# A hybrid decoder layer on one core: the cross output projection by seven block products, block sums per token tile, five early gate products, and the cross query through DRAM

## The chip, the core and the metric

The kernel runs on one core of a Trainium2 chip. The core has TensorE (PE, with the load of its stationary operand counted apart as PEld), VectorE (DVE), ScalarE (ACT) and GpSimd (POOL), each with an instruction queue that is worked off in order. SyncE (SP) issues nearly all DMAs, from one more such queue: an issue waits until its source is written and its destination is free, and what stands behind it waits too. The metric is the device time of one execution in microseconds; the time of a kernel is the median of its runs.

## What is computed

One layer of a decoder trunk on 1024 tokens of width 1024, f32, with three sub-layers, each between two RMSNorms. The change begins in the second and reaches into the third:

```python
h = h + rmsnorm(mixed @ w_out, norm_mix_post)
hn = rmsnorm(h, norm_x_pre)
qx = (hn @ w_q_x).reshape(b, s, X_HEADS, X_HEAD_DIM)              # 4 heads of 256
kx, vx = jnp.split(mn @ w_kv_x, 2, axis=-1)                        # 256 memory tokens
...
px = jax.nn.softmax(sx, axis=-1)
ox = jnp.einsum("bhsm,bmhd->bshd", px, vx).astype(h.dtype).reshape(b, s, D_MODEL)
h = h + rmsnorm(ox @ w_o_x, norm_x_post)
hn = rmsnorm(h, norm_ffn_pre)
g, up = jnp.split(hn @ w_gate_up, 2, axis=-1)                      # 2 x 2816 columns
h = h + rmsnorm((jax.nn.silu(g) * up) @ w_down, norm_ffn_post)
```

## The kernel before

**Matmuls.** Every f32 product is made of three matmuls on split operands (`mm3`, L60 to L62): high times high, high times low, low times high. `split` (L66, L75) makes the two parts of an operand tile: ACT rounds the high part, DVE subtracts it from the source. So each new operand of PE costs an ACT step and a DVE step behind it. A tile that has tokens in its rows is turned by PE transposes (`turn_in`, tiles `ptr`) and split into `A_h` and `A_l`, which hold the layer's current operand for all 1024 tokens, 8 blocks of 128 columns.

**Seven products.** Where two 2x2 block matrices are multiplied, the kernel forms seven products of sums of blocks in place of eight plain ones. Before the change the gate and up products (each pair of a gate and an up column tile is one `unit`, L1247) and the down products (L1357 on) are made so; the cross output projection isn't.

**The stages around the change**, in the order of the program:

- Query products (`qx_mm`, L996): 16 tiles `pqx` of 128 columns and 512 tokens. `qx_evac` (L1024) splits each from PSUM into `qxh` and `qxl`, which stay on the chip, as do the split keys `kxh`, `kxl` and values `vxh`, `vxl`.
- Cross attention: eight pieces (4 heads by two halves of the tokens) go through `x_scores` (`psx`, L1048), `x_soft`, `x_turn` and `x_values` (`pox`, L1080), one piece apart from step to step. `x_values` splits its result into `A_h`, `A_l`.
- Output projection (`project`, L935, with `ox_mm`, L1113): for each of the eight token tiles 48 matmuls `pwx` against the resident weight `wxh`, `wxl`. Between them stand, two tiles later each, the steps of a `Post` (L901): the sum of squares on ACT, the scaling and the add of the residual on DVE, the store of the new residual, a second norm, and then the transposes `ptr2` of the tile (`turn_ff`, L1182). Posts of tile t lie beside the matmuls of tile t+1 and t+2.
- Early gate products: the first two gate tiles (`EARLY = 2`) have 24 of their matmuls (`pga`, L1160 to L1174) while the last token tiles are still being turned.
- Block sums: `r1`, `r2` and `r3` (L1225 to L1234) form the sums R1 to R4 of the four blocks of the turned operand, for all tokens at once, when the last tile is turned; DVE, POOL and ACT do this.
- Gate stage: 22 units. The weights (`wg`, `wu`) are loaded on SP, POOL forms sums of their blocks (L1261 on), `variant` splits them, and the products `pa`, `pb`, `pc`, `pd`, `pe` follow. The results `a` and their sums `as` are stored to `act_d` (`spill`, L1302).
- Down products: seven products `pdn` with 11 steps each, whose operands are loaded from `act_d` (`ar`, L1343) and whose weights `wd` come at L1339. A last `Post` per token tile ends the program.

The order on each engine is fixed when the program is built, by a scheduler that follows the data; the code's own order is a guide to it alone. The pools limit how far an instruction can run ahead: `res` has two buffers in the second sub-layer (`bufs={1: 4, 2: 2, 3: 3}[s]`), so the residual of a token tile can be loaded when the tile two before it is done with its own.

Of the kernel before, what the change touches and what calls it, by code (L numbers as in the profile page):

```python
# [38 lines left out]
def hymba_block(tc, a, out):  # L39
# [77 lines left out]
    act_d = dram.tile([7, NF // 2, P, 512], F32, name="act_d")  # L117

# [896 lines left out]
    xq, close_xq = open_pool("xq")  # L1015
    xk, close_xk = open_pool("xk")
    qxh = [xq.tile([P, 2, T], F32R, name=f"qxh_{h}") for h in range(XH)]
    qxl = [xq.tile([P, 2, T], F32R, name=f"qxl_{h}") for h in range(XH)]
    kxh = xk.tile([P, 8, MEM], F32R, name="kxh")
    kxl = xk.tile([P, 8, MEM], F32R, name="kxl")  # L1020
    vxh = xk.tile([P, 2, D], F32R, name="vxh")
    vxl = xk.tile([P, 2, D], F32R, name="vxl")

    def qx_evac(h, half, d):  # L1024
        ts_ = slice(half * 512, (half + 1) * 512)
        split(qxh[h][:, d, ts_], qxl[h][:, d, ts_], qxp.pop((h, half, d)), scale=1.0 / 16)

    for h in range(XH):
# [171 lines left out]
    for f in range(EARLY):  # L1200
        unit_p2(f)
# [303 lines left out]
```

## Time and profile before

| | |
|---|---|
| median of three runs | 1709.34 us (1704.5 to 1712.13) |
| the profiled execution, its own time | 1712.9 us |
| its span | 1711.2 us, 22331 instructions |
| mean granted TensorE clock | 0.963 |
| PE, PEld busy | 1591.0 us (93%), 1325.6 us (77%) |
| DVE, ACT, POOL busy | 1003.4 us (59%), 735.2 us (43%), 581.7 us (34%) |
| mean DMA rate | 99 GB/s |

The span runs from the first instruction to the last; the execution's own time has some work around it. A busy share is an average over stages that differ much, so the rows that follow are taken from one stage each. All times in them are microseconds from the span's start, durations too unless ns is written.

### The profile page before, as it was taken

How to read it: one execution, taken by the hardware profiler on the slowest of the kernel's cores; microseconds unless marked ns; L12 is line 12 of the kernel's file. 1: busy time of each engine (PE TensorE's matmuls, PEld its weight loads, DVE VectorE, ACT ScalarE, POOL GpSimd, SP SyncE). 2: the span in 40 equal slices, each digit the busy share in tenths (PEclk: the TensorE clock that was granted, in tenths of full speed). 3: DMA queues.
4: the chain of work that ended last, by engine and by line, in shares of the span. 5: the costliest groups of instructions: out<-in, count | busy, mean ns of one | idle time of the engine just before them, and what ended most of it. 6: DMA issues, size and time to landing. Idle time of an engine off the chain costs nothing.

```text
span 1711.2 us, 22331 instructions
## 1 busy us (share of the span) xinstructions
PE 1591.0 (93%) x8111; PEld 1325.6 (77%) x8111; DVE 1003.4 (59%) x1653; ACT 735.2 (43%) x1474; POOL 581.7 (34%) x566
## 2 busy tenths in 40 slices
PE   7998999999999999889999964999999999599996
PEld 5796778888998888678887853888888888478885
DVE  8565455667656682773155457654445444389676
ACT  5333334446676674552264443332323322244453
POOL 5212344444554240120020028434443332188021
PEclk9999899999899999899999986999999999799999
DMA  6134111112520001532014221323322321763352
GB/s 203 50 99 154 44 50 50 38 56 87 186 98 26 20 7 46 207 125 86 1 50 148 105 92 38 110 94 120 118 99 93 108 102 49 272 235 94 113 178 99
DMA packets 65022, 168.97 MB, mean 99 GB/s; under 512 B 7568, under 2 KB 9744, under 8 KB 64912
## 3 DMA queue, kind: packets, MB, share of 16 engines
q1 hardware_dynamic: 63760, 163.35, 27.8%
q0 software_dynamic: 1152, 4.19, 0.6%
q8 instruction: 64, 1.05, 0.3%
q14 instruction: 46, 0.38, 0.1%
HBM read 124.53 MB, written 42.99 MB: 98 GB/s over the span
## 4 chain that ended last, share of the span: by engine, by line
PE 84%; DVE 7%; ACT 3%; DMA 3%; issue 2%; POOL 1%; SPq 0%; DVEq 0%; ACTq 0%; POOLq 0%
PE pv L644 5%; PE pt L626 4%; PE pdn L62 4%; PE pdn L61 4%; PE pdn L60 4%; PE pcv L60 3%; PE pcv L61 3%; PE pcv L62 3%; PE pd L62 2%; PE pd L60 2%; PE pd L61 2%; PE s L507 2%; PE pa L62 2%; PE pa L60 2%; PE pa L61 2%; PE s L508 2%
## 5 line engine op out<-in xcount | busy, mean ns | idle before, releaser
L60 PE MATMUL pdn<-wh,ah 128*128 128x512 f32 x308 | 119.9, 393 | 19.3 <-ACT wh L66 18.1
L75 DVE TENSOR_TENSOR tl<-pt,th 128x512 fp32r<-128x512 f32 (+2 forms) x168 | 102.7, 620 | 55.1 <-ACT th L66 51.2
L66 ACT ACTIVATE th<-pt 128x512 fp32r<-128x512 f32 (+2 forms) x168 | 89.7, 545 | 75.8 <-PE pv L644 38.8
L61 PE MATMUL pdn<-wl,ah 128*128 128x512 f32 x308 | 121.0, 393 | 0.4 <-DVE wl L75 0.4
L62 PE MATMUL pdn<-wh,al 128*128 128x512 f32 x308 | 118.1, 392 | 0.2 <-DVE al L75 0.2
L617 POOL TENSOR_SCALAR pw<-pw,rs,gate 128x64 f32<-128x64 f32 (+5 forms) x128 | 76.6, 609 | 119.5 <-DVE rs L615 75.8
L75 DVE TENSOR_TENSOR al<-ar,ah 128x512 fp32r<-128x512 f32 x77 | 79.1, 1032 | 45.3 <-ACT ah L66 45.3
L66 ACT ACTIVATE ah<-ar 128x512 fp32r<-128x512 f32 x77 | 48.2, 630 | 107.6 <-PE pdn L61 64.0
L617 POOL TENSOR_SCALAR ps<-ps,rs,gate 128x128 f32<-128x128 f32 (+7 forms) x64 | 53.9, 844 | 88.4 <-DVE rs L615 46.2
L60 PEld LDWEIGHTS pdn<-wh,ah 128*128 128x128 f32 x308 | 58.2, 189 | 32.3 <-ACT wh L66 18.5
L75 DVE TENSOR_TENSOR wl<-wd,wh 128x512 fp32r<-128x512 f32 x77 | 71.6, 931 | 7.7 <-ACT wh L66 7.7
L580 DVE TENSOR_REDUCE nm<-s 128x1 f32<-128x128 f32 (+7 forms) x64 | 48.0, 753 | 42.9 <-PE s L510 42.6
L1262 POOL TENSOR_TENSOR s<-wu 128x512 f32<-128x512 f32 x22 | 29.6, 1347 | 116.4 <-DVE s_8l L75 11.3
L61 PEld LDWEIGHTS pdn<-wl,ah 128*128 128x128 f32 x308 | 58.4, 190 | 13.4 <-DVE wl L75 1.2
L62 PEld LDWEIGHTS pdn<-wh,al 128*128 128x128 f32 x308 | 58.3, 190 | 12.7 <-DVE al L75 0.7
L585 DVE TENSOR_REDUCE nm<-s 128x1 f32<-128x640 f32 (+4 forms) x64 | 41.8, 653 | 44.3 <-PE s L510 44.0
L1276 DVE TENSOR_TENSOR u<-pc,u 128x512 f32<-128x512 f32 x22 | 15.2, 691 | 82.1 <-PE pc L62 82.0
L62 PE MATMUL pa<-A_h,wgl 128*128 128x512 f32 x160 | 62.9, 393 | 0.0
L60 PE MATMUL pa<-A_h,wgh 128*128 128x512 f32 x160 | 62.6, 391 | 0.0
L61 PE MATMUL pa<-A_l,wgh 128*128 128x512 f32 x160 | 62.4, 390 | 0.0
L595 ACT ACTIVATE ps<-s,nm 128x128 f32<-128x128 f32 (+7 forms) x64 | 47.4, 741 | 28.7 <-DVE nm L580 28.5
L1067 POOL TENSOR_SCALAR xe<-xe,xsm 128x256 f32<-128x256 f32 x32 | 14.8, 484 | 131.3 <-DVE xsm L1065 124.5
(1433 smaller groups left out, 5250.3 us busy)
## 6 DMA issues: line engine op xcount, KB each, us to landing
ar<-act_d SPq DMA_DIRECT2D x77, 256.0 KB, 2.7
wg<-in_w_gu_dram SPq DMA_DIRECT2D x24, 512.0 KB, 3.3
wu<-in_w_gu_dram SPq DMA_DIRECT2D x22, 512.0 KB, 3.6
act_d<-a SPq DMA_DIRECT2D x44, 256.0 KB, 2.0
wd<-in_w_down_dram SPq DMA_DIRECT2D x44, 256.0 KB, 5.4
act_d<-as_as SPq DMA_DIRECT2D x33, 256.0 KB, 2.3
h_d<-res SPq DMA_DIRECT2D x16, 512.0 KB, 2.6
res<-h_d SPq DMA_DIRECT2D x16, 512.0 KB, 4.1
```

The lines of the kernel that those rows point to most:

```text
L60: PE.matmul(ps, sh, mh, start=first, stop=False, **kw)
L61: PE.matmul(ps, sh, ml, start=False, stop=False, **kw)
L62: PE.matmul(ps, sl, mh, start=False, stop=last, **kw)
L66: ACT.activation(hi, src, AF.Copy, scale=1.0 if scale is None else scale)
L75: (DVE if lo_eng == "dve" else POOL).tensor_tensor(lo, src, f32(hi), op=ALU.subtract)
L507: PE.matmul(ps[:, cs], qh, k, start=True, stop=False)
L580: DVE.tensor_reduce(nm[:, r, 0:1], ps[:, :self.ns], axis=AX.X, op=ALU.max, negate=True)
L585: DVE.tensor_reduce(nm[:, r, 1:2], ps[:, self.w0:CM], axis=AX.X, op=ALU.max, negate=True)
L595: ACT.activation(e[:, :self.ns], ps[:, :self.ns], AF.Exp, bias=nm[:, r, 0:1], accum_out=sm[:, r, 0:1])
L617: POOL.tensor_scalar(e[:, c0:c1], e[:, c0:c1], rs[:, r, x:x + 1], gt[:, gi:gi + 1], op0=ALU.mult, op1=ALU.mult)
L626: PE.transpose(pt[:m, (2 * x + r) * P:(2 * x + r + 1) * P], self.P[b][r][:, c:c + m], ident)
L644: PE.matmul(self.pv, v, tt[:m, 256 * x:256 * x + 256], start=self.done == 1, stop=self.done == 2 * len(self.units))
```

## The change

1. **Query.** `qx_evac` copies each query tile to an f32 tile (ACT, scaled) and stores it to a DRAM tile `qx_d`. A new `x_load` loads 128x1024 of it per piece and splits it there, as it does the head's keys and values, which had been split once for all heads.
2. **Operands of the projection.** `x_values` no longer writes `A_h`, `A_l`. Per head it makes the seven split operands A11, A12, S1, S2, S4, S3 and A22 of the 2x2 block form, from three plain copies (ACT) and four sums (two on DVE, two on POOL).
3. **Projection.** `project` is replaced there by a class `Seven`, which the down products use too now: seven products of 4 steps, 48 matmuls each. The weight's blocks are loaded one by one, summed on POOL and split. Tokens 0 to 511 are complete after the fifth product, tokens 512 to 1023 after the seventh. Their posts add the residual on POOL.
4. **Block sums per token tile.** `turn_x` turns a tile and, for tiles 4 to 7, forms and splits R1 to R4 of that tile at once. The former loop over `r1`, `r2`, `r3` is gone. Tiles 0 to 3 are turned between the sixth and the seventh product.
5. **Early gate products.** `EARLY` is 5. Each `early_unit` loads its own two half weights, makes 24 matmuls `pea`, and stores the two results to a DRAM tile `early_d`, from which `unit` loads them. `turn_x` of tiles 4 to 7 stands between the units.

The core of the diff (the rest of `Seven` is the down stage's code with other names; `posts`, `slot` and the pools are left out):

```diff
     def qx_evac(h, half, d):
-        ts_ = slice(half * 512, (half + 1) * 512)
-        split(qxh[h][:, d, ts_], qxl[h][:, d, ts_], qxp.pop((h, half, d)), scale=1.0 / 16)
+        e = qw.tile([P, 512], F32, tag="ev", name=f"qe_{h}_{half}_{d}", bufs=4)
+        ACT.activation(e, qxp.pop((h, half, d)), AF.Copy, scale=1.0 / 16)
+        SP.dma_start(qx_d[h, half, :, d, :], e)
...
+    def x_load(h, tq):
...
+        SP.dma_start(raw, qx_d[h, tq])
+        split(hi, lo, raw)
+        qs[h, tq] = hi, lo
...
-            split(A_h[:, 2 * h + d, ts_], A_l[:, 2 * h + d, ts_], po)
+            if tq == 0:
+                keep_o(("o11", "o12")[d], po)
+                put((A11, A12)[d], h, po)
+            elif d == 0:
+                keep_o("o21", po)
+            else:
...
+                DVE.tensor_tensor(s1, po, o21, op=ALU.add)
+                put(A22, h, po)
+                DVE.tensor_tensor(s2, s1, o11, op=ALU.subtract)
+                put(S2, h, s2)
+                put(S1, h, s1)
+                POOL.tensor_tensor(o12, o12, s2, op=ALU.subtract)
+                put(S4, h, o12)
+                POOL.tensor_tensor(o21, o11, o21, op=ALU.subtract)
+                put(S3, h, o21)
...
-    project(2, ox_mm, ox_evac, lambda t: h1_d[t], h2_d, ox, g_post, g_next, gu_early, turn_ff)
...
+    EARLY = 5
...
+    def turn_x(t, m):
...
+        ACT.activation(c12, pts[0], AF.Copy)
+        DVE.tensor_tensor(r1, pts[0], f32(h11), op=ALU.subtract)
+        DVE.tensor_tensor(r1, r1, f32(l11), op=ALU.subtract)
+        put_x("22", 2, cs, pts[1])
+        DVE.tensor_tensor(r3, pts[1], c12, op=ALU.subtract)
+        DVE.tensor_tensor(r2, pts[1], r1, op=ALU.subtract)
+        put_x("R2", 4, cs, r2)
+        POOL.tensor_tensor(r2, f32(h21), r2, op=ALU.subtract)
+        put_x("R1", 3, cs, r1)
+        POOL.tensor_tensor(r2, f32(l21), r2, op=ALU.add)
+        put_x("R3", 5, cs, r3)
+        put_x("R4", 6, cs, r2)
...
+    def early_unit(f):
...
+            SP.dma_start(raw, a["w_gu"][f][:, x * H:(x + 1) * H, :])
+            split(hi, lo, raw)
...
+        for x, (b, fn) in enumerate((("11", AF.Copy), ("21", AF.Silu))):
+            product(ps, w[x], b, x == 1)
+            e = ox_raw(f"ee{x}_{f}")
+            ACT.activation(e, ps, fn)
+            SP.dma_start(early_d[x, f], e)
...
+    def ox_done(t):
+        posts[t] = Post(ox, 2, t, y2[t], g_post, h1_d[t], h2_d[t], g_next)
+        posts[t].add(POOL)
+        posts[t].norm()
+
+    def ox_between(n):
+        if n == 5:
+            for t in range(4):
+                turn_x(t, posts[t].m)
...
+    for f in range(EARLY):
+        early_unit(f)
+        if f < 4:
+            turn_x(4 + f, posts[4 + f].m)
...
         if f < EARLY:
-            g = gu.tile([P, NK, P], F32, tag="raw", name=f"wg2_{f}", bufs=4)
-            SP.dma_start(g, a["w_gu"][f])
+            SP.dma_start(m1, early_d[0, f])
+            SP.dma_start(sg1, early_d[1, f])
```

What the scheduler makes of it shows in the order of instructions on three places.

**DVE, the norms of the first token tiles.** Before, the steps of one tile stand together (m2 is the projected tile, res2 its residual, ss2 its factors); at tiles 5 and 6:

```order
L85 RECIPROCAL ss2_5_9356<-ss2_5_9356 128x1
L914 SCALAR_TENSOR_TENSOR m2_5_9354<-m2_5_9354,ss2_5_9356,g_post2_8924 128x1024
L915 TENSOR_TENSOR res2_5_9357<-res2_5_9357,m2_5_9354 128x1024
L85 RECIPROCAL ss2_5_9356<-ss2_5_9356 128x1
L922 SCALAR_TENSOR_TENSOR m2_5_9354<-res2_5_9357,ss2_5_9356,g_next2_8926 128x1024
L75 TENSOR_TENSOR A_l_95<-ptr2_4_1_9422,A_h_94 128x4x128
L85 RECIPROCAL ss2_6_9434<-ss2_6_9434 128x1
L914 SCALAR_TENSOR_TENSOR m2_6_9432<-m2_6_9432,ss2_6_9434,g_post2_8924 128x1024
L915 TENSOR_TENSOR res2_6_9435<-res2_6_9435,m2_6_9432 128x1024
L85 RECIPROCAL ss2_6_9434<-ss2_6_9434 128x1
L922 SCALAR_TENSOR_TENSOR m2_6_9432<-res2_6_9435,ss2_6_9434,g_next2_8926 128x1024
```

Now, from the third row behind tile 0's second scaling on, which follows the fifth product (y2 holds the projected tile, xp5 is the sixth product, xl6 the low part of the seventh product's weight, x11 and x21 the turned tile):

```order
L75 TENSOR_TENSOR xl6_2_9679<-xw10_2_9675,xh6_2_9678 128x512
L1228 TENSOR_TENSOR y2_6_9055<-xp5_2_9519,y2_6_9055 128x512 x2
L1228 TENSOR_TENSOR y2_7_9056<-xp5_3_9520,y2_7_9056 128x512 x2
L85 RECIPROCAL ss2_2_9488<-ss2_2_9488 128x1
L75 TENSOR_TENSOR xl6_3_9686<-xw10_3_9682,xh6_3_9685 128x512
L85 RECIPROCAL ss2_1_9473<-ss2_1_9473 128x1
L75 TENSOR_TENSOR x11_l_9608<-ptr2_0_0_9597,x11_h_9607 128x4x128
L75 TENSOR_TENSOR x21_l_9612<-ptr2_0_1_9602,x21_h_9611 128x4x128
L85 RECIPROCAL ss2_3_9503<-ss2_3_9503 128x1
L916 SCALAR_TENSOR_TENSOR y2_2_9051<-y2_2_9051,ss2_2_9488,g_post2_9045 128x1024
L924 SCALAR_TENSOR_TENSOR y2_1_9050<-res2_1_9474,ss2_1_9473,g_next2_9047 128x1024
L916 SCALAR_TENSOR_TENSOR y2_3_9052<-y2_3_9052,ss2_3_9503,g_post2_9045 128x1024
```

The steps of tiles 0 to 3 are interleaved now, and between tile 0's second scaling and tile 1's (next to last row) stand the sixth product's eight sums, two of the seventh product's weight splits and tile 0's two splits.

**ACT and SP, from the last token tile to the gate stage.** Before, ACT has two early Silu steps and then the splits of the block sums (r is a sum, R2h and R3h their high parts):

```order
L1174 ACT_TABLE_LOAD
L1174 ACTIVATE sg1_0_9610<-pga_0_9542 128x512
L1174 ACTIVATE sg1_1_9624<-pga_1_9570 128x512
L1195 ACTIVATE b12_8872<-ptr2_7_0_9585 128x4x128
L66 ACTIVATE A_h_94<-ptr2_7_1_9591 128x4x128
L66 ACTIVATE R3h_9636<-r_0_2_9645 128x512
L66 ACTIVATE A_h_94<-r_0_0_9643 128x512
L66 ACTIVATE R3h_9636<-r_1_2_9663 128x512
L66 ACTIVATE R2h_9634<-r_0_1_9644 128x512
```

Now, around the second and third early unit (pea is a unit's product, ee its two results, ew its weight, xr the sums of a turned tile):

```order
L1322 ACTIVATE ee0_1_9906<-pea_1_9893 128x512
L1322 ACT_TABLE_LOAD
L1322 ACTIVATE ee1_1_9921<-pea_1_9893 128x512
L1289 ACTIVATE xr0_5_9934<-ptr2_5_0_9924 128x512
L66 ACTIVATE xR3_h_9873<-xr3_5_9937 128x4x128
L66 ACTIVATE xR1_h_9868<-xr1_5_9935 128x4x128
L66 ACTIVATE xR2_h_9863<-xr2_5_9936 128x4x128
L66 ACTIVATE ew0h_2_9956<-ew0_2_9955 128x512
L66 ACTIVATE ew1h_2_9962<-ew1_2_9961 128x512
```

Each unit's weight splits (last two rows) stand behind the unit before and behind three splits of the turned tile's sums. On SP, before:

```order
L916 DMA h2_d_66<-res2_5_9357 128x1024
L908 DMA res2_7_9513<-h1_d_65 128x1024
L916 DMA h2_d_66<-res2_6_9435 128x1024
L916 DMA h2_d_66<-res2_7_9513 128x1024
L1251 DMA wg2_0_9727<-in_w_gu_dram 128x1024
L1256 DMA wu_0_9729<-in_w_gu_dram 128x1024
```

Now, from the fourth early unit on:

```order
L1323 DMA early_d_69<-ee0_3_10054 128x512
L1323 DMA early_d_69<-ee1_3_10069 128x512
L1315 DMA ew0_4_10103<-in_w_gu_dram 128x512
L1315 DMA ew1_4_10109<-in_w_gu_dram 128x512
L1323 DMA early_d_69<-ee0_4_10128 128x512
L1323 DMA early_d_69<-ee1_4_10143 128x512
L1362 DMA wg_0_10157<-in_w_gu_dram 128x1024
L1363 DMA wu_0_10158<-in_w_gu_dram 128x1024
L1367 DMA m1_0_10161<-early_d_69 128x512
```

The next unit's weight stands behind the store of the results of the unit before, and the first gate and up weights stand behind the last unit's stores.

**SP, from the gate stage to the down products.** Before (act_d is the store of results, ar their load, res3 a residual, wd a weight):

```order
L1303 DMA act_d_67<-a01_10_12598 128x512
L1343 DMA ar_0_2_12966<-act_d_67 128x512
L1303 DMA act_d_67<-as_as4_10_12882 128x512
L1343 DMA ar_0_3_12990<-act_d_67 128x512
L908 DMA res3_0_14274<-h2_d_66 128x1024
L908 DMA res3_1_14285<-h2_d_66 128x1024
L908 DMA res3_2_14296<-h2_d_66 128x1024
L1343 DMA ar_0_4_13014<-act_d_67 128x512
L1343 DMA ar_0_5_13038<-act_d_67 128x512
L1339 DMA wd_00_0_12916<-in_w_down_dram 128x512
```

Now:

```order
L910 DMA res3_0_14623<-h2_d_66 128x1024
L1413 DMA act_d_67<-as_as1_10_13231 128x512
L910 DMA res3_1_14634<-h2_d_66 128x1024
L1413 DMA act_d_67<-a10_10_12950 128x512
L1413 DMA act_d_67<-as_as2_10_13232 128x512
L910 DMA res3_2_14645<-h2_d_66 128x1024
L1413 DMA act_d_67<-a01_10_12949 128x512
L1413 DMA act_d_67<-as_as4_10_13233 128x512
L1170 DMA dw00_0_13261<-in_w_down_dram 128x512
L1445 DMA ar_0_0_13265<-act_d_67 128x512
```

The residual loads have moved from between the last spill and the first weight to between the spills.

## Rows read from the trace of the kernel before

**Rows 1.** The longest waits of PE: engine, line, releaser: us in total, times, longest.

```profile
PE pb L60 <- ACT s_0h L66: 38.0, 1, 38.0
PE pdn L60 <- ACT wh L66: 18.1, 1, 18.1
```

**Rows 2.** Stretches: us, busy PE, PEld, DVE, ACT, POOL, granted clock, DMA share, GB/s.

```profile
844.00:903.00 59.00, 55.33 (x354) 49.17 (x352) 31.84 (x49) 34.44 (x99) 14.78 (x32) 0.97 0.11 39
903.00:1000.00 97.00, 95.01 (x428) 77.23 (x429) 46.43 (x55) 42.74 (x71) 0.00 (x0) 0.98 0.34 124
1013.00:1051.00 38.00, 0.43 (x4) 0.19 (x2) 28.55 (x29) 11.27 (x20) 28.36 (x19) 0.55 0.11 42
1077.00:1460.00 383.00, 383.00 (x1675) 314.26 (x1674) 185.36 (x257) 112.24 (x174) 147.71 (x114) 1.00 0.28 98
```

**Rows 3.** Groups of 844 to 903: busy us, mean ns, then idle before and releaser.

```profile
L75 DVE TENSOR_TENSOR A_l<-pox,A_h 128x512 fp32r<-128x512 f32 x16 | 10.8, 688 | 6.7 <-ACT A_h L66 6.6
...
L66 ACT ACTIVATE A_h<-pox 128x512 fp32r<-128x512 f32 x16 | 9.6, 614 | 8.4 <-PE pox L62 8.4
```

**Rows 4.** Timeline, 848 to 850 and 897 to 1006: start, us, instruction, times, idle before.

```profile
848.55 1.28 ACT L1063 ACT_TABLE_LOAD   x1 [3.58 <-DVE xnm L1060]
...
849.85 0.47 ACT L1063 ACTIVATE xe<-psx,xnm 128x256 f32<-128x256 f32 x1
...
897.98 1.28 DVE L75 TENSOR_TENSOR xtl<-ptx,xth 128x512 fp32r<-128x512 f32 x2
...
1001.70 1.07 ACT L910 ACTIVATE scr<-m 128x1024 bf16<-128x1024 f32 x1
...
1002.90 0.29 ACT L84 ACTIVATE ss<-ss,eps 128x1 f32<-128x1 f32 x1
...
1003.26 1.03 PE L1192 MATMUL ptr<-ident,m 128*128 128x128 f32 x8
...
1003.42 1.28 DVE L914 SCALAR_TENSOR_TENSOR m<-m,ss,g_post 128x1024 f32<-128x1024 f32 x1
...
1004.75 1.23 DVE L915 TENSOR_TENSOR res<-res,m 128x1024 f32<-128x1024 f32 x1
```

**Rows 5.** Timeline at 719: an add on POOL beside a scaling on DVE.

```profile
719.09 2.40 POOL L915 TENSOR_TENSOR res<-res,mixed 128x1024 f32<-128x1024 f32 x1 [2.56 <-DVE ss L85]
...
719.19 3.38 DVE L922 SCALAR_TENSOR_TENSOR mixed<-res,ss,g_next 128x1024 f32<-128x1024 f32 x1
```

**Rows 6.** DMA issues: transfer, queue, times, KB each, us to landing.

```profile
ar<-act_d SPq DMA_DIRECT2D x77, 256.0 KB, 2.7
...
wu<-in_w_gu_dram SPq DMA_DIRECT2D x22, 512.0 KB, 3.6
act_d<-a SPq DMA_DIRECT2D x44, 256.0 KB, 2.0
wd<-in_w_down_dram SPq DMA_DIRECT2D x44, 256.0 KB, 5.4
...
res<-h_d SPq DMA_DIRECT2D x16, 512.0 KB, 4.1
```

**Rows 7.** Stretches as in rows 2: a gap of PE and what follows it.

```profile
748.00:751.40 3.40, 0.94 (x5) 0.97 (x6) 3.40 (x5) 2.56 (x6) 1.16 (x1) 0.87 0.38 154
751.40:754.80 3.40, 3.40 (x13) 2.87 (x12) 3.40 (x7) 1.20 (x2) 0.00 (x0) 0.63 0.00 0
```

**Rows 8.** Timeline, from the last gate matmul to the first down matmul.

```profile
1464.61 0.40 PE L62 MATMUL pd<-R4h,a_21l 128*128 128x512 f32 x1
...
1468.82 1.26 POOL L1320 TENSOR_TENSOR as_as<-a,as_as 128x512 f32<-128x512 f32 x1
...
1472.04 1.58 SPq L908 DMA_DIRECT2D res<-h_d  x3
...
1475.80 5.56 SPq L1339 DMA_DIRECT2D wd<-in_w_down_dram  x7
...
1483.07 2.08 PE L60 MATMUL pdn<-wh,ah 128*128 128x512 f32 x4 [18.06 <-ACT wh L66]
```

More of the change, by code (lines that the diff above doesn't have):

```diff
@@ L1188, in turn_ff, with x_slot, put_x @@
+    XV = {}
+    def x_slot(n, x):
+        if x not in XV:
+            XV[x] = slot(n, f"x{x}_")
+        return XV[x]
+    def put_x(x, n, cs, src):
+        v = x_slot(n, x)
+        split(v[0][:, :, cs], v[1][:, :, cs], src)
+    def turn_x(t, m):
+        cs = slice(t % 4 * P, (t % 4 + 1) * P)
+        pts = []
         for half in range(2):
-            pt = ps_a(f"ptr2_{t}_{half}")
+            pt = ps_f(f"ptr2_{t}_{half}")
             for c in range(4):
@@ L1255, in unit @@
-        u = gu.tile([P, NK, P], F32, tag="raw", name=f"wu_{f}", bufs=4)
-        SP.dma_start(u, a["w_gu"][f + NF])
+            SP.dma_start(m1, early_d[0, f])
+            SP.dma_start(sg1, early_d[1, f])
+        else:
+            hi = gu.tile([P, NK, P], F32R, tag="gh", name=f"wgh_{f}", bufs=2)
+            lo = gu.tile([P, NK, P], F32R, tag="gl", name=f"wgl_{f}", bufs=2)
+            split(hi, lo, g)
+            pa = ps_f(f"pa_{f}")
+            product(pa, (hi[:, :H, :], lo[:, :H, :]), "11")
+            ACT.activation(m1, pa, AF.Copy)
@@ L1270, in unit @@
         if f >= EARLY:
-            unit_p2(f)
-        v1 = variant(f"s1_{f}", s1)
+            product(pa, (hi[:, H:, :], lo[:, H:, :]), "21", True)
+            ACT.activation(sg1, pa, AF.Silu)
         pc = ps_f(f"pc_{f}")
-        product(pc, v1, "R1")
+        product(pc, variant(f"s1_{f}", s1), "R1")
         u4 = gt.tile([P, 512], F32, tag="u4", name=f"u4_{f}", bufs=1)
@@ L1332, in hymba_block, with post, __getitem__ @@
+    def post(t):
+        p = Post(dn, 3, t, y3[t], g_post, h2_d[t], out[t * P:(t + 1) * P, :], None)
+        p.add(DVE if t == NT - 1 else POOL)
+    y3 = {}
+    class Rows:
+        def __getitem__(self, t):
+            if t not in y3:
+                y3[t] = dk.tile([P, D], F32, name=f"y3_{t}")
+            return y3[t]
     g_post = dn.tile([P, D], F32, name="g_post3")
     SP.dma_start(g_post, row_bcast(a["norm_ffn_post"]))
-    y = [dk.tile([P, D], F32, name=f"y_{t}") for t in range(NT)]
@@ L1392, in r3 @@
-    def r3(j):
-        POOL.tensor_tensor(wd[0, 1, j], wd[1, 1, j], wd[0, 1, j], op=ALU.subtract)
-    def r4(j):
-        POOL.tensor_tensor(wd[1, 0, j], wd[1, 0, j], wd[0, 0, j], op=ALU.subtract)
-    def post(i):
-        p = Post(dn, 3, i, y[i], g_post, h2_d[i], out[i * P:(i + 1) * P, :], None)
-        p.add(DVE if i == NT - 1 else POOL)
-    for i, ps in enumerate(down_product(0, w_plain(0, 0))):
-        ACT.activation(X1[i], ps, AF.Copy)
-    for i, ps in enumerate(down_product(1, w_plain(1, 0))):
-        DVE.tensor_tensor(y[i][:, :512], ps, X1[i], op=ALU.add)
```

384 lines of the change are left out of this document (170 added, 214 removed).

## The prediction

> **What bounds the kernel now.** I first asked who TensorE (PE) waits for [rows 1]. Two waits stand out: 38.0 us before the first gate product (pb) for a split on ACT, and 18.1 us before the first down product (pdn). The busy time by stretch [rows 2] then shows what kind of stage the change enters: cross attention from 844 to 903 (PE busy 55.3 of 59), the output projection from 903 to 1000 (95.0 of 97), the hole from 1013 to 1051, in which PE does nothing while DVE and POOL work 28 us each, and the gate stage, where PE is busy 383.0 of 383. That last row gives the matmul's price: 383.0 / 1675 = 0.229 us. So the stages that the change touches are PE's own, but the two holes are not: there a chain of small steps on ACT, DVE, POOL and the SP queue sets the time. The change has to be priced in both currencies: matmuls, which it saves, and links of such chains, which it adds.
>
> **Cross attention.** Its query now goes out to DRAM and is split again on return, keys and values are split per head, and each head gives seven split operands, not four. From 844 on that adds to ACT six 128x1024 splits (1.06 each, as the square of that size in [rows 4]), four key and value splits, twelve plain copies and twelve splits at 0.61 [rows 3]: 6.4 + 28 x 0.61 = 23.4, on 34.4 now [rows 2], so 57.8 of 59. DVE gets 6 x 1.23 [rows 4] + (4 + 12 + 8) x 0.69 [rows 3] = 23.9 on 31.8, so 55.7. POOL gets eight sums of 1.26 [rows 8]. PE keeps its matmuls. Bounds: nothing is lost if all of it hides (both still fit), 12 us if half of the added work doesn't. I take 3, nearer to the first, because both sums are under 59. The first output product also needs the operands of all heads, and ACT's queue puts its first weight split behind the last head's sums: two DVE steps (1.4), two POOL sums (2.5) and two ACT splits (1.2) after the last attention matmul, 5.1 where about 2 pass now. First matmul at 903 + 3 + 3 = 909, and once the low half of the weight is there too, products flow as if from 910. The DRAM trip itself I cost at nothing: the 92 us of query products before 844 cover it, and only the last pieces come back late; without that cover it is 2.0 + 4.1 us [rows 6] per piece.
>
> **The projection.** Seven products of 48 matmuls replace 384: 48 x 0.229 = 11.0 saved. Products one to five take 55.0, to 965; the sixth ends at 976. Their operand work (per product 4 splits, 4 to 8 sums on DVE and 4 sums on POOL, in 11 us of PE) hides.
>
> Then comes what I hold to be the **price**. Tokens 0 to 511 are finished by the fifth product; their transposes stand on PE behind the sixth and ahead of the seventh, and the order of the queues makes their four norms nearly serial. Counted from 965, with the steps of [rows 4]: sum 0.7, two squares 2.5, table load 1.3, root and reciprocal 0.5, scaling 1.3, add on POOL 2.4 [rows 5] (1.23 on DVE now), square, root, reciprocal 1.7, scaling 1.3: tile 0 turns at 11.7, as the sixth product ends (11.0). But next in DVE's queue are the sixth product's eight sums and the last two weight splits (10 x 0.64 = 6.4), then tile 0's two splits (1.3), then tile 2's scaling (1.3), and only then tile 1's second scaling (1.3): tile 1 turns at 21.5. Tile 3's residual takes the buffer of tile 1 (there are two), so its load goes out then: 4.1 [rows 6], add 2.4, norm 3.0, transposes 1.0: the seventh product starts at 965 + 32 = 997, where PE was free at 976 (bounds 27, if no step meets another, and 36, see the third rival). It ends at 1008, and 1 us goes to the lower clock after the gap: after 4.0 idle us the next stretch was granted 0.63 of the clock and held 13 matmul records [rows 7]. So the projection ends at 1009, now at 1000: the 11 us are gone, and 9 with them.
>
> **From there to the gate stage.** Now 51.4 us [rows 2]. New: five early units with 24 matmuls each (5.5 us) and a turn (1.03) in each of the first four. The first ends 9 us after the projection: 6.5 of work and a wait for tile 4's norm. The second unit's weight split stands in ACT's queue behind tile 7's second square, whose residual waits for tile 5's buffer, for its load (4.1) and POOL's add (2.4): it starts at 17 and ends at 24. Units three to five are a loop, link by link: the unit before ends; 0.9 later its Silu is done and SP can store it, and behind that store stands the next weight's load, 2.0 to 2.7 until landing [rows 6]; in parallel ACT copies the turned tile (0.5), DVE forms three sums (1.9), ACT splits the last of them (0.6) and only then the weight (0.5): 4.4 after the unit's end. Two matmuls, the turn and 22 matmuls take 6.6. That is 11.0, of which PE works 6.5; with half a us of low clock 11.5, three times: 58.5. After the last unit SP stores its Silu first and then issues the first gate and up weights: 0.9 + 0.3 + 3.6 [rows 6], two POOL sums 2.5, a split 0.6: 7.9 to the first gate matmul. With 3 us for starts at the low clock, 69.4 in all, so the gate stage starts at 1078.4 instead of 1051.4: **+27.0**.
>
> **What comes back.** In the gate stage three more units have two of their products behind them: 72 x 0.229 = **-16.5**. On the way to the down products SP now has three 512 KB residual loads ahead of the first down weight: last POOL sum at 1468.8, residuals 1472.0, weight issued only at 1475.8, PE at 1483.1, 18.1 after its last matmul [rows 8]. In the new order the residuals go out between the spills, and the weight right behind the last spill, 5.6 after the last matmul; with 3.7 to land (between 2.0 and 5.4 [rows 6]) and two splits of 0.65 PE starts after 10.6: **-7.5**. The rest, 228 us, is the same matmuls and sums in nearly the same order.
>
> **Sum.** 27.0 - 16.5 - 7.5 = +3.0 us on an execution of 1712.9 us (span 1711.2). It lies 3.6 above the median of the runs, 1709.3; on the median the forecast is **1712 us**, +0.2%: no change that a measurement of this kernel can tell, for which I take 0.5%, 8.5 us.
>
> **Two rules against the trace.** A table load takes 1.28 us, and the next activation starts right behind it, 1.30 after [rows 4]. The Trainium skill, "ScalarE: Activation LUTs", section "What ACT_TABLE_LOAD costs", gives 2.66 us with a drain. By the page the four loads of the new chain would add 4 x 1.38 = 5.5 us and the sum would be 1718; the trace shows no such drain.
> In [rows 5] an add on POOL and a scaling on DVE start 0.1 us apart, and the scaling takes 3.38 instead of 1.28 us: it waits for POOL's 2.40. The Trainium skill, "SBUF — State Buffer", section "SBUF: two separate sides", says the two share a port that is locked for a whole instruction. The trace agrees. What it would do here is the third rival.
>
> **Rivals.**
> *The queues are looser than I read them (faster).* The seventh product starts after 27, the tail takes 60, attention loses nothing: 5 + 9 + 3 less, 1695. For it: DVE and POOL are far from full between 903 and 1000. Against: each queue is in order, and two chains (the weight's load and the sums) give the loop the same 4 us.
> *The holes are really filled (faster).* The early units cover the hole as a count of matmuls suggests: the 38.0 us fall to about 5, with 11.0 and 7.5 saved and 6 lost in attention: 1709 - 33 - 11 - 7 + 6 = 1664. Against: every unit needs what the one before it ends with.
> *POOL's adds hold DVE (slower).* Eight 2.4 us adds and eight 1.3 us sums lie on POOL among DVE's scalings and splits, ahead of PE's turns. If each blocks a DVE step, as in [rows 5], tile 3 turns 4 later, the second unit starts 2 later, the loop takes 13 (+4.5 over three), and gaps of 6 us cost 1.2 more of clock in each of four units: 1712 + 15 = 1727. It decides where DVE's splits in the loop take over 1 us each.
> *Attention runs full (slower).* ACT at 57.8 of 59 cannot keep up with PE: 12 instead of 3, 1721.
>
> **Chances and range.** My case 0.44 (its own range 1701 to 1717); the looser queues 0.19 and the filled holes 0.05; POOL's adds 0.20, full attention 0.12. So faster by over 0.5% 0.24, within it 0.44, slower 0.32. From the looser queues with every landing at 2.0 (1693) to POOL's adds with attention's loss beside them (1734) about 1 in 5 is left out.
>
> **What would show it.** Right: the wait before pb falls from 38.0 to about 8; a new wait of 16 to 20 us in all stands before the transposes (ptr) of the first four tiles, and three waits of 4 to 5 us before pea; the first gate matmul comes at 1078 within 8; the first wait of the down stage is near 11. Wrong: PE busy through from 976 to the gate stage (then the holes are filled), or an attention stage that still runs at 912.

## The result: 1.4% slower, and where the time went

The changed kernel takes **1732.8 us** (median of four runs, 1730.5 to 1738.7) beside 1710.7 of the kernel before on the same chips: ratio 1.0137, 95% interval 1.0095 to 1.0179. The forecast was 1712 and no change. The time lies inside the range (1693 to 1734), but the likeliest case was wrong. The profiled execution took 1730.5 us, its span is 1728.5.

I cut both traces at the same events and count from the first score matmul of cross attention (`psx`), which comes at 844.2 before and 840.4 now; up to some 750 us the two programs are the same, and there the changed one was already 5.0 ahead, so the lead is scatter between executions (1.2 of it went in the query products, whose first matmuls stayed longer at the lower clock). "First early product" is the first matmul of the early gate products. The projection's own last matmul ends close to it, at 155.6 before and 164.8 now. All in us:

| | first output product | first early product | first gate product | gate stage | down stage with the wait ahead of it | sum |
|---|---|---|---|---|---|---|
| before | 59.0 | 156.2 | 207.2 | 413.6 | 246.2 | 867.0 |
| changed | 62.9 | 164.6 | 245.5 | 397.4 | 245.2 | 888.1 |
| difference | +3.9 | +8.4 | **+38.3** | -16.2 | -0.9 | +21.1 |

The first three columns are points in time, the next two lengths. The differences are taken before rounding. The 21.1 fits the medians' 22.1.

The longest waits of PE in the changed kernel (engine, line, releaser: us in total, times, longest):

```profile
PE pea L60 <- ACT ew0h L66: 24.5, 4, 9.1
PE dp L60 <- ACT ah L66: 15.4, 2, 14.2
PE ptr L1281 <- DVE y L924: 15.4, 3, 7.8
PE pb L60 <- ACT s_0h L66: 9.9, 1, 9.9
...
PE xp L60 <- ACT xh L66: 5.1, 1, 5.1
```

The 38.0 us before the first gate product [rows 1] are 9.9, as the fill was meant to have it. But the filling itself now waits: 24.5 us for early weights, 15.4 ahead of the transposes of tiles 0 to 3. The stretches (us, busy PE, PEld, DVE, ACT, POOL, granted clock, DMA share, GB/s) of the first six products, the gap ahead of the seventh, the tail to the first gate product, and the gate stage:

```profile
903.30:971.30 68.00, 67.98 (x288) 55.56 (x288) 38.56 (x52) 23.59 (x40) 27.07 (x18) 0.96 0.25 88
971.30:994.00 22.70, 7.26 (x32) 6.07 (x33) 21.79 (x29) 10.41 (x24) 6.17 (x3) 0.55 0.40 141
...
1005.20:1085.90 80.70, 41.78 (x153) 31.13 (x151) 45.25 (x59) 35.60 (x64) 24.32 (x14) 0.79 0.37 128
1085.90:1483.30 397.40, 397.35 (x1728) 325.62 (x1728) 209.80 (x279) 117.02 (x182) 171.59 (x127) 1.00 0.31 105
```

Six products run without a gap (68.0 of 68.0). Then come 22.7 us with 32 transposes in them, and 80.7 us that hold 153 records. In the first of these DVE is nearly full (21.8 of 22.7); in the second no engine is. The granted clock is 0.55 and 0.79.

One early unit follows from the timeline (start, us, instruction, times, idle before). The third unit ends at 1047.1:

```profile
1047.18 0.60 ACT L1322 ACTIVATE ee<-pea 128x512 f32<-128x512 f32 x1 [3.17 <-PE pea L62]
...
1048.22 0.87 SPq L1315 DMA_DIRECT2D ew<-in_w_gu_dram  x2
...
1049.62 1.95 ACT L66 ACTIVATE xR_h<-xr 128x512 fp32r<-128x512 f32 x3 [1.35 <-DVE xr L1293]
...
1051.51 0.63 ACT L66 ACTIVATE ew0h<-ew 128x512 fp32r<-128x512 f32 x1
...
1053.21 1.91 PE L1281 MATMUL ptr<-ident,y 128*128 128x128 f32 x8
```

Silu, store, the weight's load at 1048.2: with its median of 3.4 to landing it is there at about 1051.6. ACT finishes three splits of the turned tile's sums at 1051.6, and its weight split begins at 1051.5. Two chains end in the same tenth of a microsecond. Then PE runs at the lower level (1.2 GHz), as the granted clock of 0.50 of the 2.6 us behind the gap says: the eight transposes take 1.91 where they took 1.03 [rows 4].

```profile
1052.19:1054.77 2.58, 2.58 (x10) 2.28 (x11) 2.58 (x3) 0.58 (x1) 1.90 (x2) 0.50 0.02 6
```

### The profile page after: what moved, and what is told of

Its sections match the earlier page's. It is cut to its first block, busy times and chain, and to the rows that moved or that the text cites. A ratio compares the mean times of both kernels' runs of the same rounds, so it can differ in the third digit from the quotient of the medians.

```text
span 1728.5 us, 22611 instructions
## 1 busy us (share of the span) xinstructions
PE 1589.0 (92%) x8063; PEld 1320.5 (76%) x8063; DVE 1052.6 (61%) x1722; ACT 761.0 (44%) x1533; POOL 635.5 (37%) x590
## 3 DMA queue, kind: packets, MB, share of 16 engines
q8 instruction: 63, 1.03, 0.2%
## 5 line engine op out<-in xcount | busy, mean ns | idle before, releaser
L75 DVE TENSOR_TENSOR tl<-pt,th 128x512 fp32r<-128x512 f32 (+2 forms) x168 | 102.7, 620 | 55.5 <-ACT th L66 53.6
L60 PE MATMUL dp<-dh,ah 128*128 128x512 f32 x308 | 119.9, 393 | 15.4 <-ACT ah L66 15.4
L61 PE MATMUL dp<-dl,ah 128*128 128x512 f32 x308 | 120.3, 394 | 1.7 <-DVE dl L75 1.7
L62 PE MATMUL dp<-dh,al 128*128 128x512 f32 x308 | 117.7, 392 | 0.8 <-DVE al L75 0.8
L917 POOL TENSOR_TENSOR res<-res,y 128x1024 f32<-128x1024 f32 x15 | 40.6, 2714 | 150.6 <-DVE y L916 103.5
L75 DVE TENSOR_TENSOR dl<-dw,dh 128x512 fp32r<-128x512 f32 x77 | 76.6, 996 | 20.4 <-ACT dh L66 20.3
L1174 POOL TENSOR_TENSOR dw<-dw,dw 128x512 f32<-128x512 f32 x44 | 73.0, 1686 | 35.2 <-DMA dw<-in_w_down_dram 31.2
L619 POOL TENSOR_SCALAR ps<-ps,rs,gate 128x128 f32<-128x128 f32 (+7 forms) x64 | 53.6, 838 | 87.8 <-DVE rs L617 46.4
L60 PEld LDWEIGHTS dp<-dh,ah 128*128 128x128 f32 x308 | 58.2, 190 | 28.4 <-ACT ah L66 16.3
L582 DVE TENSOR_REDUCE nm<-s 128x1 f32<-128x128 f32 (+7 forms) x64 | 47.9, 753 | 40.1 <-PE s L512 39.9
L61 PEld LDWEIGHTS dp<-dl,ah 128*128 128x128 f32 x308 | 58.4, 190 | 16.2 <-DVE dl L75 4.0
L62 PEld LDWEIGHTS dp<-dh,al 128*128 128x128 f32 x308 | 58.2, 190 | 13.5 <-DVE al L75 1.6
L587 DVE TENSOR_REDUCE nm<-s 128x1 f32<-128x640 f32 (+4 forms) x64 | 41.8, 653 | 41.4 <-PE s L512 41.0
L1081 POOL TENSOR_SCALAR xe<-xe,xsm 128x256 f32<-128x256 f32 x32 | 21.8, 698 | 116.0 <-DVE xsm L1079 111.5
L66 ACT ACTIVATE dh<-dw 128x512 fp32r<-128x512 f32 x77 | 47.7, 620 | 35.0 <-PE dp L62 20.6
```

Of the source, the lines that this page charges most:

```text
L60: PE.matmul(ps, sh, mh, start=first, stop=False, **kw)
L61: PE.matmul(ps, sh, ml, start=False, stop=False, **kw)
L62: PE.matmul(ps, sl, mh, start=False, stop=last, **kw)
L66: ACT.activation(hi, src, AF.Copy, scale=1.0 if scale is None else scale)
L75: (DVE if lo_eng == "dve" else POOL).tensor_tensor(lo, src, f32(hi), op=ALU.subtract)
L582: DVE.tensor_reduce(nm[:, r, 0:1], ps[:, :self.ns], axis=AX.X, op=ALU.max, negate=True)
```

## Experiments

Every kernel was timed beside the kernel before on the same chip; the first early and the first gate product are counted from psx as above, the gate stage is a length. In e9 to e12 the four turns of tiles 0 to 3 stand between the projection and the first early product.

| | us | against before, 95% | first early product | first gate product | gate stage |
|---|---|---|---|---|---|
| changed | 1732.8 | 1.0095 to 1.0179 | 164.6 | 245.5 | 397.4 |
| e1 loads ahead | 1717.3 | 1.0029 to 1.0068 | 166.2 | 232.7 | 398.5 |
| e2 two units | 1721.8 | 1.0054 to 1.0112 | 164.7 | 222.9 | 414.9 |
| e3 adds on DVE | 1728.2 | 1.0079 to 1.0133 | 161.1 | 242.1 | 397.4 |
| e4 gaps filled | 1727.1 | 1.0085 to 1.0133 | 166.1 | 242.5 | 396.0 |
| e5 query alone | 1710.0 | 0.9973 to 1.0022 | 155.9 | 206.9 | 414.0 |
| e6 room for gate weights | 1726.4 | 1.0094 to 1.0135 | 167.6 | 239.9 | 395.9 |
| e7 three residuals | 1739.5 | 1.0157 to 1.0205 | 169.6 | 254.2 | 397.7 |
| e8 units in halves | 1705.1 | 0.9967 to 1.0001 | 166.0 | 219.6 | 398.1 |
| e9 turns behind seventh | 1735.2 | 1.0117 to 1.0166 | 162.6 | 246.4 | 398.5 |
| e10 halves, DVE, behind | 1696.3 | 0.9902 to 0.9932 | 154.5 | 210.6 | 397.5 |
| e11 and room | 1697.1 | 0.9904 to 0.9941 | 157.5 | 210.5 | 398.6 |
| e12 and seven units | **1688.5** | 0.9858 to 0.9915 | 157.4 | 215.3 | 384.9 |

**e1, the loads one unit ahead.**

```diff
...
+    early_load(0)
     for f in range(EARLY):
+        if f + 1 < EARLY:
+            early_load(f + 1)
+        early_split(f)
         early_unit(f)
```

> The loads of an early unit's weight are written one unit ahead, before the matmuls of the unit before it; the splits stay in the code where they were, right ahead of their own unit. In the trace of the changed kernel the third early unit's weight lands at 1051.5 and ACT's queue reaches its split at 1051.5 too. Theory (two chains of equal length, and the scheduler moves the split up once the load is early): the four waits before pea (24.5 us) go, a unit costs 24 x 0.229 + 1.03 + 0.7 = 7.2, the first gate product comes near 1052 in place of 1085.9, 1705 us. Rival A (ACT's queue alone holds the unit, the splits stay behind the sums): waits of 4.4, 1729. Rival B (DVE sets the pace: 11 steps of 0.69 and what collides with POOL, some 11 us a unit): 1717.

Measured: 1717.3, the figure of rival B, but not by its mechanism: DVE is busy 44.8 of the 66.3 us from the first early product to the first gate product. The waits for ew0h are gone, so taking the load from behind the stores was enough to end them, and ACT's place in the queue followed it (with the load early, the scheduler puts the split early too). But a new wait took their place:

```profile
PE ptr L1281 <- DVE y L924: 17.9, 4, 7.8
...
PE pea L60 <- ACT ee L1333: 14.9, 4, 8.0
PE pb L60 <- ACT s_0h L66: 11.1, 1, 11.1
```

`ee` is ACT's copy of a unit's first half, which PE has to let pass before it adds the second half onto the same tile of PSUM, the memory in which PE accumulates. ACT's timeline shows what this copy stands behind:

```profile
1027.65 0.63 ACT L66 ACTIVATE xR_h<-xr 128x512 fp32r<-128x512 f32 x1 [4.09 <-POOL xr L1298]
...
1033.77 0.58 ACT L1333 ACTIVATE ee<-pea 128x512 f32<-128x512 f32 x1
...
1034.97 0.61 ACT L66 ACTIVATE ew0h<-ew 128x512 fp32r<-128x512 f32 x1
```

ACT idles 4.1 us until POOL has formed R4 of the tile; in its queue the copy stands behind that split, with six instructions between them.

**e2, two early units.**

```diff
-    EARLY = 5
+    EARLY = 2
...
+    for f in range(4):
+        if f < EARLY:
+            early_unit(f)
+        turn_x(4 + f, posts[4 + f].m)
```

> Two early units in place of five, everything else as in the changed kernel. Theory (each of the last three units costs its period of 14.3 us in the tail and gives back 24 x 0.229 = 5.5 in the gate stage): -43 + 16.5 = -26, 1706 us, first gate product near 1042. Rival (the gate stage waits for the norms and sums of tiles 6 and 7, which the units merely lie beside): no sooner than 1065, -4 in all, 1728.

Measured: 1721.8, between the theory and the rival. The first gate product comes 22.6 sooner than in the changed kernel, not 43, and the gate stage takes 17.5 more. Of the three units' 43 us, 20 lay beside work that the gate stage waits for anyway. What it waits for shows on SP and DVE, behind a wait of 29.7 us:

```profile
1046.12 0.33 SPq L1362 DMA_DIRECT2D wg<-in_w_gu_dram  x1
...
1050.52 0.69 DVE L75 TENSOR_TENSOR xR_l<-xr,xR_h 128x512 fp32r<-128x512 f32 x1 [3.15 <-ACT xR_h L66]
1051.24 0.33 SPq L1363 DMA_DIRECT2D wu<-in_w_gu_dram  x1
```

Nothing is in front of the gate weights on SP, and yet `wu` goes out right when the last sum is split. Its buffer lies where the tail's buffers lay; e6 takes it out of there.

**e3, the adds of the posts on DVE.**

```diff
-        posts[t].add(POOL)
+        posts[t].add(DVE)
```

> The residual adds of the second sub-layer's posts on DVE in place of POOL. Theory (the queues hold the turns; POOL's 2.4 to 3.3 us per add become 1.23 on DVE, which has other steps too): the seventh product starts some 2 us sooner and the second unit 1 to 2, 1729 us. Rival (the adds on POOL hold DVE's scalings and splits, as the 3.38 us scaling at 983.5 and the 5.70 us for two splits at 966.7 say): 6 to 8 us sooner at the seventh product, 3 at the second unit, 1722.

Measured: 3.5 us sooner at the first early product, and 3.4 at the first gate product; 1728.2, near the theory's 1729, though the two ratios' intervals overlap. The collision is there in the changed kernel's trace:

```profile
982.56 3.28 POOL L917 TENSOR_TENSOR res<-res,y 128x1024 f32<-128x1024 f32 x1 [10.70 <-DVE y L916]
983.53 3.38 DVE L916 SCALAR_TENSOR_TENSOR y<-y,ss,g_post 128x1024 f32<-128x1024 f32 x1
```

The scaling ends 1.07 behind POOL's add: it waits for it, as in [rows 5]. This agrees with the Trainium skill, "SBUF — State Buffer", section "SBUF: two separate sides", by which the two engines share a port under a lock. But all eight adds together are worth 4 us here, not the 15 of my third rival, probably since few of them meet a DVE step that PE waits for; that reason isn't tested.

**e4, the gaps filled with idle matmuls.** Their results go unused.

```diff
             SP.dma_start(early_d[x, f], e)
+        n = {0: 32, EARLY - 1: 36}.get(f, 16)
+        for k in range(n):
+            PE.matmul(ps, w[0][0][:, k % H, :], XV["11"][0][:, k % H, :], start=k == 0, stop=k == n - 1)
```

> Extra matmuls (32, 16, 16, 16, 36) behind the five early units, into the PSUM tile that the unit has done with, from operands that lie there: they stand in the gaps in which PE waits for the next weight (9.1, 5.0, 5.1, 5.3, 9.9 us), 0.7 us behind the unit's end; their result isn't used. Theory (a unit takes 9.1 us and not 7.2 because the clock is low after each gap): units of 7.2, -1.9 x 4 and some 2 at the gate stage's start, 1723 us, granted clock of 1005 to 1086 over 0.95 where it was 0.79. Rival (a unit's length is set by its operands, its low parts late): units stay at 9 us, 1733.

The clock came up as expected, from 0.79 to 1.00:

```profile
1006.80:1083.20 76.40, 61.53 (x270) 46.31 (x268) 45.50 (x60) 35.54 (x64) 24.80 (x14) 1.00 0.39 134
```

From the first early product to the first gate product it took 76.4 in place of 80.9, and the runs 5.7 less, not some 10. A unit with its turn still takes 8.0 (9.1 in the changed kernel): the copy of the first half is now waited for 1.1 to 1.4 us, where slow matmuls hid part of it. The start of one unit follows that of the one before at 13.3 (26.6 from the second to the fourth), where it took 14.9 (29.7): the lower clock costs 1.6 us per unit, with the longer wait for the copy already taken off.

**e5, the query through DRAM alone, on the kernel before** (`qx_evac` and `x_load` as in the change, the rest as before).

> The kernel before with one part of the change alone: the query goes through DRAM and is split per piece, keys and values are split per head; output projection and all behind it as before. Theory (92 us of query products cover the trip, and ACT's and DVE's added splits, 10.4 and 7.4 + 2.8 us, fit in a stage of 59): attention takes 57 to 58 from psx to the last pox, as before, 1710 us, within 3. Rival (ACT and DVE run full and pieces come late): 61 or more, 1714.

1710.0, ratio 0.9997; first gate product at 206.9 (207.2); attention even ended 2.0 sooner (57.0 to the first output product), which a wait for the output weight took back. This part of the change costs nothing and gains nothing. So the 3.9 by which the first output product is later in the changed kernel belong to the seven operands and the weight's queue, not to the query.

**e6, the gate's weight buffers in the room of tiles 0 to 3.**

```diff
+    yr, close_yr = open_pool("yr")
...
-    y2 = [ox.tile([P, D], F32, name=f"y2_{t}") for t in range(NT)]
+    def big(name):
+        return yr.tile([P, D], F32, tag="raw", name=name, bufs=4)
+
+    y2 = [big(f"y2_{t}") if t < 4 else ox.tile([P, D], F32, name=f"y2_{t}") for t in range(NT)]
+    def raw_tile(name):
+        return big(name).rearrange("p (k m) -> p k m", k=NK)
...
+    gate_load(0)
+    gate_load(1)
     for f in range(EARLY):
         early_unit(f)
...
-    def tile_raw(name):
-        return gu.tile([P, NK, P], F32, tag="raw", name=name, bufs=4)
```

> The changed kernel, with the gate stage's four raw weight buffers in the room of the projected tiles 0 to 3, which are done with by 994, and not in that of the projection's pool: the first four gate and up weights are loaded behind the seventh product. Theory (the first gate product waits 9.9 us because the weight's load can go out only when the early units' buffers are free, and lands 4.9 later): 3.1 to 6 us are left (two POOL sums, a split), and the load of the first unit stands at about 990; 1727 us. Rival (the gate stage waits for something else of the last unit, its stores or the last sums): still 9, 1732. On SP the three residual loads now come behind the first down weights: if they slowed these (6.4 us to landing), the 14.2 us before the first down product fall to 12; if not, they stay.

The wait before the first gate product fell from 9.9 to 1.25, further than expected: POOL forms the weight's sums while the last unit runs.

```profile
1075.58 1.59 POOL L1393 TENSOR_TENSOR s<-s,wg 128x512 f32<-128x512 f32 x1
...
1081.15 0.50 PE L60 MATMUL pb<-xR_h,s_0h 128*128 128x512 f32 x1 [1.25 <-ACT s_0h L66]
```

The edit gives the load free room and also puts it ahead of the units on SP, so this run alone doesn't tell the two apart; that the room holds such a load shows in e2, where nothing stood ahead of `wu` on SP. Of the 8.6 us that the wait lost, 5.6 are left at the first gate product: the first output product came 2.3 later (65.2 against 62.9), as ACT waited 2.15 for the output weight's load, and the first early product 2.9. The second half of the run is a lesson of its own. The first down weight goes out 0.1 us before the gate stage's end and lands after 3.9 us, with the residual loads behind it (6.4 behind the end, and after 6.4, in the changed kernel). The first down product now starts 5.8 us behind the gate stage, not 14.2, and still the wait and the down stage together take 245.9. The first 17 us of the down stage, in the changed kernel and then here:

```profile
1497.45:1514.45 17.00, 17.00 (x65) 13.86 (x66) 11.53 (x18) 10.46 (x17) 0.00 (x0) 0.86 1.05 387
```

```profile
1482.80:1499.80 17.00, 14.41 (x54) 11.13 (x55) 7.63 (x13) 6.30 (x12) 0.00 (x0) 0.91 1.04 379
```

All DMA engines are busy in both; started sooner, PE starves inside the product. Over all fourteen kernels the two lie between 244.5 and 246.3 together, whatever the wait. The Trainium skill, "DMA: Bandwidth & Descriptors", section "Where 436 GB/s comes from", gives some 358 GB/s per core for traffic with the DRAM and 435 for the fabric. The 387 measured here is above the first and below the second, so 358 was no bound in this run. The rate itself was not varied, so that it is the limit is read from the rows alone; a rival, that the loads go out late because their buffers come free late, is tested by no run.

**e7, three residual buffers.**

```diff
-            self.res = pool.tile([P, D], F32, tag="res", name=f"res{s}_{t}", bufs={1: 4, 2: 2, 3: 3}[s])
+            self.res = pool.tile([P, D], F32, tag="res", name=f"res{s}_{t}", bufs={1: 4, 2: 3, 3: 3}[s])
...
-            self.scr = pool.tile([P, D], BF, tag="scr", name=f"scr{s}_{t}", bufs=2)
+            self.scr = pool.tile([P, D], BF, tag="scr", name=f"scr{s}_{t}", bufs=1 if s == 2 else 2)
```

> Three residual buffers in the second sub-layer in place of two (and one for the square's unused output in place of two, to make room). Theory (tile 3's residual waits for tile 1's buffer, tile 7's for tile 5's): tile 3's load goes out 8 us sooner, the seventh product starts 3 sooner and the second unit 3; 1727 us. Rival (DVE's queue holds tiles 1 and 3, loads or not): 0 at the seventh product, 1732.

Slower by 6.7: an experiment spoilt by its second line. A tile's square writes `scr`, and so does its second square, behind the add; with one buffer the next tile's norm can't begin until this one's is done. Tile after tile, 7 us apart:

```profile
977.94 2.72 POOL L917 TENSOR_TENSOR res<-res,y 128x1024 f32<-128x1024 f32 x1 [9.81 <-DVE y L916]
...
985.23 2.35 POOL L917 TENSOR_TENSOR res<-res,y 128x1024 f32<-128x1024 f32 x1 [4.56 <-DVE y L916]
...
992.20 2.35 POOL L917 TENSOR_TENSOR res<-res,y 128x1024 f32<-128x1024 f32 x1 [4.62 <-DVE y L916]
```

What the third buffer does alone stays open. The run shows what wholly serial norms cost, less whatever the third buffer gives: 5 us at the end of the projection.

**e8, units in halves.**

```diff
...
     for f in range(EARLY):
-        early_unit(f)
+        if f + 2 < EARLY:
+            early_load(f + 2)
+        if f + 1 < EARLY:
+            early_half(f + 1, 0)
+        early_half(f, 1)
         if f < 4:
             turn_x(4 + f, posts[4 + f].m)
+        if 0 < f < 5:
+            r4s.pop(0)()
```

> Early weights loaded two units ahead; PE makes the first half of the next unit ahead of the second half of this one; the two POOL sums and the split for R4 of a tile stand one unit later. Theory (with the loads ahead, PE waited 14.9 us in all for ACT's copy of a half unit, which stood in ACT's queue behind splits whose sums come from DVE and POOL): these waits fall below 5, five units in some 45 us, first gate product 57 us behind the projection's end in place of 66 with the loads ahead alone; 1707 us. Rival (what holds PE is tile 6's and 7's norms, through their transposes, so that a wait for ptr takes the place): 1715, as with the loads ahead alone.

1705.1, the theory's 1707 and 27.7 less than the changed kernel; 0.9984 of the kernel before, which can't be told from no change. From the first early product on the tail fell from 80.9 to 53.6 (245.5 - 164.6; 219.6 - 166.0). The waits that are left (the three for ptr are those of tiles 0 to 3):

```profile
PE ptr L1282 <- DVE y L924: 16.4, 3, 8.7
...
PE pb L60 <- ACT s_0h L66: 11.7, 1, 11.7
...
PE pea L60 <- ACT ew0h L66: 6.6, 2, 4.3
```

**e9, the first four turns behind the seventh product.**

```diff
-        if n == 5:
+        if n == 6:
             for t in range(4):
```

> The changed kernel with the transposes of tiles 0 to 3 behind the seventh product in place of ahead of it. Theory (PE stands 22 us ahead of the seventh product only because these transposes, whose norms are nearly serial, are queued in front of it): the seventh product runs right behind the sixth, 11 us sooner to its end by 22; the first early unit needs the four tiles and starts at about 997 in place of 1005, and the norms of tiles 4 to 7 are no later than now: -8, 1725 us. Rival (DVE's queue sets the turns, and the seventh product's sums and the next norms come into it ahead of tiles 1 to 3): the fourth tile is turned at 1003 or later, -2, 1731.

The seventh product ran behind the sixth, as meant, and the first unit began 2.0 sooner, not 8; the second one started later, and 1735.2 is no gain: the rival.

```profile
PE pea L60 <- ACT ew0h L66: 26.6, 4, 11.2
...
PE ptr L1281 <- DVE y L924: 12.5, 2, 8.2
```

PE's stall ahead of the seventh product was a true wait, but nothing was lost by it: the second unit hangs on the norms of tiles 4 to 7, in the same queues. DVE's is the full one: from 978 to 1003 of this trace it is busy 24.2 of 25.0 us.

**e10 and e11, the three together, and the gate weights' room besides.** Edits as in e8, e3 and e9; e11 also as in e6.

> The units in halves (1705 us), with the adds on DVE (-4 where it was tried on the changed kernel) and the first four turns behind the seventh product (-8 by theory). If the three are independent: 1693 us. If DVE's queue is the bound behind all three: 1701 to 1705.

> As e10, with the gate stage's first weights in the room of tiles 0 to 3, too, which are now turned later. Theory: the wait before the first gate product falls from some 11 to 2 to 4 us as it did alone (9.9 to 1.3); what the wait before the down products loses is given back in the first down product, as there: 1687 us. Rival (tiles 0 to 3 give their room only behind the seventh product, and DVE's last sums hold the gate stage): no difference to e10.

e10: 1696.3, near the 1693 of independent gains. The first early product comes 11.5 us sooner than in e8, where the adds alone gave 3.5 (e3) and the turns alone 2.0 (e9). So the edits pay more together than apart; which of them brings the rest is not separated. DVE is the full engine of this stretch: from the sixth product's end to the first early product it is never idle.

```profile
971.00:994.84 23.84, 16.17 (x80) 13.68 (x80) 23.84 (x39) 14.06 (x32) 0.00 (x0) 0.82 0.36 127
```

e11 takes the same time as e10, but not because the room did nothing. The first output product comes 3.7 later, as it came later in e6; the wait before the first gate product falls from 13.1 to 9.9, and the two cancel. What is left of the wait is the rival: POOL forms tile 7's last sums, behind DVE, and goes on at once to the weight's.

```profile
1043.89 1.64 POOL L1302 TENSOR_TENSOR xr<-x_h,xr 128x512 f32<-128x512 f32 x1 [1.83 <-DVE xR_l L75]
1045.61 1.26 POOL L1303 TENSOR_TENSOR xr<-x_l,xr 128x512 f32<-128x512 f32 x1
1046.83 1.27 POOL L1413 TENSOR_TENSOR s<-wu 128x512 f32<-128x512 f32 x1
```

**e12, seven units.** `EARLY = 7` in e11.

> As e11, with seven early units in place of five. In e11 PE stands 9.9 us between the last unit and the first gate product, while POOL forms tile 7's last sums (two of 1.6 and 1.3) and then the gate weight's two. Theory (this wait is work of other engines, and two more units, 11 us, lie in it): the first gate product comes 1 to 4 us later than in e11, the gate stage is 11 us shorter, 1688 us. Rival (POOL's, ACT's and SP's queues put the units' steps ahead of the last sums, so that the wait is pushed back): first gate product 8 us or more later, 1695.

**1688.5**, 1.1% faster than the kernel before and, by the two ratios, 2.5% faster than the changed one. The first gate product comes 4.8 later than in e11, a little over the 1 to 4 expected, and the gate stage is 13.7 shorter. The tail:

```profile
992.70:1050.60 57.90, 47.90 (x201) 37.77 (x201) 48.46 (x69) 39.71 (x73) 20.04 (x12) 0.89 0.51 185
```

PE works 47.9 of 57.9 us, where it worked 41.8 of 80.7.

## Why the prediction was wrong

By its own terms, in the order of the program:

- **To the end of the projection, +9 forecast, +9.2 measured (its last matmul ends 155.6 and 164.8 behind psx): right**, and for the reason given. The seventh product started 153.6 us behind psx where 152.8 was forecast; the waits before ptr sum to 15.4 (16 to 20 forecast). Attention lost 3.9 to the first output product, not 6: its last matmul came 0.4 later, not 3, and then 5.1 us pass, as forecast. That the end fits to a tenth is luck: the six products took 68.0 where 66 was forecast, the stall 22.7 and not 21 (tile 1 turns at 22.0 by the steps listed, not 21.5), the seventh product 11.2 and not 12, and with the earlier start these cancel. I had read the stall as one of order in DVE's queue; DVE is busy 21.8 of its 22.7 us, so its work sets it too. e9 adds what the step did not see: this stall hides behind the norms of the later tiles and is worth nothing alone.
- **The tail, +18.0 forecast (69.4 against 51.4), +29.1 measured (80.7 against 51.6, from the projection's last matmul): the step that failed.** The list of links was right but for one that was missing, and their sizes were not. The second unit began 17.3 behind the projection (17 forecast) but took 10.1, not 7; three units took 43.4, not 34.5; the gate weights 9.9, not 7.9; the 3.0 that I had set aside for starts at the low clock is in these figures. That makes 3.4 + 8.9 + 2.0 - 3.0 = 11.3. The 8.9 of the three units have three parts. PE's own matmuls and turns took 25.8, where I had 19.8 and 1.5 for the lower clock: 4.5. The gaps between the units are 15.4, not 13.2, as the load lands after 3.4 and not 2.0 to 2.7: 2.2. And the copy between a unit's halves, a link that I had put at nothing, is waited for 2.2 (e1 and e8 show how much it can be). e4 bears out the clock's part: with PE kept busy the three units take 39.8, 3.6 less, although the copy is then waited for 3.8. Most of the last 2.0 is the up weight's load, which went out 1.7 behind the last unit's end and landed after 4.7, where I had 1.2 and 3.6; that it could go out long before, given room and an earlier place on SP, shows in e6.
- **The gate stage, -16.5 forecast, -16.2 measured: right**: 72 matmuls at the price of [rows 2].
- **The way to the down products, -7.5 forecast: wrong.** The wait fell by 3.9 (18.1 to 14.2), since the load landed after 6.4 and not 3.7 (3.9 in e6, where the residual loads come later); and the down stage gave 2.9 of it back, so that -0.9 is left. The step took a wait for a price without asking what the next product needs from the DRAM.

Sum: +9.2 + 29.1 - 16.2 - 0.9 = +21.2, where I had +3.0.

The rivals: that POOL's adds hold DVE gave 1727, near the result, but by a mechanism that is worth 4 us alone (e3); a number near the measured one is no proof of a cause. Full attention (+12) didn't happen. The filled holes (1664 by a count of matmuls) are not reached even with five edits beyond the change, at 1688. The Trainium skill, "ScalarE: Activation LUTs", section "What ACT_TABLE_LOAD costs", counts a drain beside each table load. The trace shows none here either: a load of 1.28 us at 1018.23 was followed by the root at 1019.52.

## What to carry to other kernels

Work moved into a hole counts as filling only if its own inputs are there: write down, for each small unit, which store, load and evacuation of the unit before it stands ahead in each queue, and price the period of that loop, with the low clock after its gap. Several chains can end at nearly the same time, as here, so taking one away brings out the next; look for the second before expecting the first one's full price. Look for a full engine in each short stretch, too: one with room to spare over the stage can be full in the 20 us that count, as DVE was. And a wait at a stage's start is worth something only where the stage behind it isn't short of the same thing.

## What was not expected of the hardware

- The wait before the down stage could be cut from 14.2 to 5.8 us without any gain, with DMA shares of 1.04 to 1.05 and 379 to 387 GB/s in the 17 us behind it (e6).
- A gap of 5 us in PE's work costs more than the gap: the granted clock was 0.50 in the 2.6 us behind one, and keeping PE busy (e4) gave back 1.6 us per unit of 24 matmuls and 8 transposes; the transposes alone took 0.9 more (1.91 against 1.03).
